# Moving a split store from batch 11 to batch 2 in a batched matmul

## The chip, the core and the metric

The kernel runs on one core of one Trainium2 chip. The metric is device time in microseconds of one execution; lower is better. Sixteen DMA engines serve the core and carry all traffic between its on-chip memory and HBM. Transfers are put on three queues: ACT's (q10 in the profile), SP's (q1) and GpSimd's, called POOL here (q0).

## The reference

```python
batch, m, k, n = 16, 512, 512, 512
a: (batch, m, k) float32, b: (batch, n, k) float32
np.matmul(a, b.transpose(0, 2, 1)).astype(np.float32)
```

Sixteen products of 512 x 512 matrices, each with its second matrix transposed. 33.5 MB are read and 16.8 MB written.

## The kernel before

The batches are worked on in eight pairs. One load brings the two matrices `a` of a pair, the next the two matrices `b`, 2 MB each, into one of `NL = 7` slots of `ld`: 128 partitions, one run of 16 KB in each. Loads 0, 2, 3, ... are put on ACT's queue and load 1 on SP's (`load`, line 86). The first seven go out at the start; ACT issues loads 7 and 8 after its copies `ta` of pair 0, loads 9 and 10 after those of pair 1, and so on.

For each pair DVE casts the halves of `a` and `b` to bf16 (`ha`, `wa`, `hb`, `wb`), PE transposes them in blocks of 128 x 128 into PSUM (`tp`, line 223), ACT copies the transposed `a` to `ta` (line 181) and DVE the transposed `b` to `tb` (line 168). PE multiplies (line 242), and ACT copies the product from PSUM to one of `NO = 7` slots of `ob` (line 201). DVE doesn't wait for a load itself: POOL waits for each load in turn and counts up `s_go` (line 108), and DVE takes one from this count for each load. So whatever stands between two of POOL's waits stands between DVE and the next load.

SP stores the batches in order. It first waits until load 7 has landed (line 120, the second use of slot 0), then for each batch until ACT has copied it (`s_out`), and puts one transfer of 1 MB on its queue: 128 partitions, a run of 8 KB in each (`store`, line 96). ACT waits for the store of batch n - 7 before it writes batch n into the same slot of `ob` (`landed`, line 93, and line 198). The last 256 KB of batch 15 are a transfer of their own at the very end.

One batch is stored in another way, `X = 11`. Of its four rows `j` in each partition, SP stores rows 1 and 2 of all partitions, rows 0 and 3 of partitions 32 to 95, and rows 0 and 3 of partitions 0 to 19 in five transfers of four partitions. POOL, after its last wait for a load, stores rows 0 and 3 of partitions 20 to 31 and 96 to 127 in four rounds of three transfers (lines 112 to 118). Each round begins with a small load of 640 bytes to a scratch tile, `turn`, of five partitions with two runs of 64 bytes, and goes on with a store of three partitions and one of eight. The pieces count on `s_x` (SP's) and `s_y` (POOL's), for which ACT waits at the very end.

Of the kernel before, what the change touches and what calls it, by code (L numbers as in the profile page):

```python
# [10 lines left out]
def kernel(  # L11
# [6 lines left out]
    nc = tc.nc  # L18
    P = 128
    batch, M, K = a.shape  # L20
    _, N, _ = b.shape
    J = M // P
    KO = K // P
    HP = P // 2
    HK = K // 2
    pairs = batch // 2
    f32 = mybir.dt.float32
    bf16 = mybir.dt.bfloat16
    NL = 7
    NO = 7  # L30
    X = 11

    def sbuf(name, shape, dtype):
        return ctx.enter_context(nc.sbuf_tensor(name, shape, dtype))

    def sem(name):
        return tc.alloc_semaphore(name)

    with tc.tile_critical(no_gpsimd_drain=True):  # L41
# [6 lines left out]
        ta = sbuf("ta", [P, KO, 2 * J * P], bf16)  # L48
        tb = sbuf("tb", [P, KO, 2 * J * P], bf16)
        ob = sbuf("ob", [P, NO, J, N], f32)  # L50
        turn = sbuf("turn", [P, 4, 2, 16], f32)
        tp = ctx.enter_context(nc.psum_tensor("tp", [P, 4, 2 * J, P], bf16))
        ps = ctx.enter_context(nc.psum_tensor("ps", [P, 4, N], f32))

# [2 lines left out]
        s_st = [sem(f"s_st{i}") for i in range(NO)]  # L57
# [13 lines left out]
        s_out = sem("s_out")  # L71
        s_x = sem("s_x")
        s_y = sem("s_y")
# [5 lines left out]
            out=ident[:], in_=ident[:], compare_op=mybir.AluOpType.not_equal, fill=1.0,  # L79
# [6 lines left out]
        def load(n, engine):  # L86
            u, slot = n // 2, n % NL
            src = (a if n % 2 == 0 else b)[2 * u:2 * u + 2].rearrange(
                "e (p j) k -> (e p) j k", j=2 * J
            )  # L90
            engine.dma_start(ld[:, slot], src).then_inc(s_ld[slot], 16)

        def landed(n):
            return s_st[n % NO], 16 * (n // NO + 1)

        def store(n, lo=0, hi=J, step=1, part=slice(0, P), engine=nc.sync):
            rows = slice(lo, hi, step)
            return engine.dma_start(  # L98
                out[n].rearrange("(p j) n -> p j n", j=J)[part, rows], ob[part, n % NO, rows]
            )  # L100

        load(0, nc.scalar)
# [3 lines left out]

        for n in range(2 * pairs):
            nc.gpsimd.wait_ge(s_ld[n % NL], 16 * (n // NL + 1)).then_inc(s_go, 1)

        nc.gpsimd.wait_ge(s_out, X + 1)
        for i in range(4):
            nc.gpsimd.dma_start(  # L114
                turn[:5, i], a[0, :5, :64].rearrange("p (x k) -> p x k", x=2)[:, :, :16]
            ).then_inc(s_y, 16)
            for part in (slice(20 + i, 32, 4), slice(96 + i, P, 4)):
                store(X, step=J - 1, part=part, engine=nc.gpsimd).then_inc(s_y, 16)

        nc.sync.wait_ge(s_ld[0], 32)  # L120
        for n in range(batch):
            nc.sync.wait_ge(s_out, n + 1)
            if n != X:
                store(n, hi=J if n < batch - 1 else J - 1).then_inc(landed(n)[0], 16)
                continue


            store(n, lo=1, hi=J - 1).then_inc(landed(n)[0], 16)
            store(n, step=J - 1, part=slice(32, 96)).then_inc(s_x, 16)
            for i in range(4):  # L130
                store(n, step=J - 1, part=slice(i, 16, 4)).then_inc(s_x, 16)
            store(n, step=J - 1, part=slice(16, 20)).then_inc(s_x, 16)

        def taker(engine):
            return lambda s, n: engine.wait_ge(s, n).then_inc(s, -n)  # L135
# [9 lines left out]
        with nc.Fori(0, pairs, engines=[dve]) as u:  # L145
            for x, (h, w, s_c, s_w) in enumerate(
# [4 lines left out]
                if x == 0:  # L151
# [4 lines left out]
                    out=h[:, J:, :], in_=src[:, J:, :HK]  # L156
                ).then_inc(s_c, 1)
                nc.vector.tensor_copy(out=w[:], in_=src[:, :, HK:]).then_inc(s_w, 1)  # L158
            for ko in range(KO):
# [5 lines left out]
                if ko == 1:  # L165
# [3 lines left out]
                    out=tb[:, ko, :],  # L169
# [7 lines left out]
        for u in range(pairs):  # L177
            for ko in range(KO):
                nc.scalar.wait_ge(s_ta, KO * u + ko + 1)
                for e in range(2):  # L180
                    c = nc.scalar.copy(  # L181
                        out=ta[:, ko, e * J * P:(e + 1) * J * P].rearrange(
                            "k (j p h) -> k j p h", j=J, h=2
                        ),
                        in_=tp[:, ko % 2, :, e * HP:(e + 1) * HP].rearrange(
                            "k (h j) p -> k j p h", h=2
                        ),
                    )
                c.then_inc(s_ea, 1)


            for n in (2 * u + NL, 2 * u + NL + 1):
                if n < 2 * pairs:
                    load(n, nc.scalar)
            for e in range(2):
                n = 2 * u + e
                if n >= NO:
                    nc.scalar.wait_ge(*landed(n - NO))
                for j in range(J):
                    nc.scalar.wait_ge(s_mm, J * n + j + 1)  # L200
                    c = nc.scalar.copy(  # L201
                        out=ob[:, n % NO, j, :].rearrange("m (p j) -> m p j", j=2 * J),
                        in_=ps[:, j, :].rearrange("m (j p) -> m p j", j=2 * J),
                    )
                    if e == 0:
                        c.then_inc(s_pv, 1)
                    elif j in (0, J - 1):
                        c.then_inc(s_out, 1)
# [45 lines left out]


    with tc.tile_critical(sync_engine=act, no_gpsimd_drain=True):
        nc.scalar.wait_ge(s_x, 16 * 6)
        nc.scalar.wait_ge(s_y, 16 * 12)
        for n in range(batch - NO, batch):
            nc.scalar.wait_ge(*landed(n))  # L260
    waits = nc.cur_bb.bb.instructions[-1]
# [38 lines left out]
```

## Time and profile before

| | |
|---|---|
| median of 9 runs | 125.01 us (124.77 to 125.44) |
| the profiled execution | 125.01 us |
| its span | 123.2 us |
| PE, DVE, ACT, POOL busy | 91.4, 68.0, 67.9, 8.5 us |
| packets of DMA | 50.35 MB, mean 409 GB/s |
| q10, q1, q0 | 31.46, 18.70, 0.18 MB |
| load 15 counted by POOL | 100.19 us |
| SP issues store 15 | 115.04 us |
| last packet of DMA ends | 121.61 us |

Times within an execution are counted from the start of the span. The page cuts the span in 40 slices of 3.08 us; a digit is the busy share of a slice in tenths. A row of a timeline gives its start, its length, engine, line, operation, what it writes and reads, how many were merged, and in brackets the idle time before it and what ended that. "ACTq" and "SPq" are issues of transfers, which take the issuing engine's time and not that of the transfer.

### The profile page before, as it was taken

The numbers are of one execution on the slowest core, as the hardware profiler recorded it, in microseconds if no ns is written. First come the engines' busy times: TensorE is split into PE (matmuls) and PEld (weight loads), VectorE is DVE, ScalarE is ACT, GpSimd is POOL, SyncE is SP. The second block draws the span as 40 slices with busy tenths as digits, with TensorE's granted clock in tenths as the row PEclk, the third lists the DMA queues.
The fourth block names the chain that finished last, engine by engine and source line by source line (L and its number), as shares of the span: only waits on it lengthen the run. The fifth ranks groups of instructions, "written<-read, shape, count | busy, mean of one in ns | idle before, by whom it ended". The sixth has DMA issues, their size and how long they took to land. (4 is left out here: it accounts for less than half of the span.)

```text
span 123.2 us, 2255 instructions
## 1 busy us (share of the span) xinstructions
PE 91.4 (74%) x768; PEld 56.1 (46%) x768; DVE 68.0 (55%) x96; ACT 67.9 (55%) x130; POOL 8.5 (7%) x18
## 2 busy tenths in 40 slices
PE   0000089999999899989998999999699926999100
PEld 0000078347744764674476447645564425844000
DVE  0000598983895689289918974871987039600000
ACT  0400065468855966796589469765765184645300
POOL 2000000000000000000000000000000029930000
PEclk9999999999999999999999999999999999599965
DMA  4999999999999999999999999999999999999992
GB/s 149 415 426 426 442 426 426 431 426 426 426 426 426 436 340 388 428 439 420 434 431 420 444 423 426 447 420 412 444 428 436 412 426 426 419 405 425 426 420 104
DMA packets 5341, 50.35 MB, mean 409 GB/s; under 512 B 904, under 2 KB 904, under 8 KB 1500
## 3 DMA queue, kind: packets, MB, share of 16 engines
q10 hardware_dynamic: 2160, 31.46, 60.7%
q1 hardware_dynamic: 2796, 18.70, 36.2%
q0 software_dynamic: 384, 0.18, 0.5%
q14 instruction: 1, 0.01, 0.0%
HBM read 33.56 MB, written 16.78 MB: 409 GB/s over the span
## 5 line engine op out<-in xcount | busy, mean ns | idle before, releaser
L242 PE MATMUL ps<-tb,ta 128*128 128x512 bf16 x256 | 58.1, 381 | 0.4
L201 ACT COPY ob<-ps 128x512 f32<-128x512 f32 x64 | 34.3, 590 | 27.4 <-PE ps L242 23.5
L181 ACT COPY ta<-tp 128x512 bf16<-128x512 bf16 x64 | 33.0, 613 | 15.5 <-PE tp L223 15.1
L242 PEld LDWEIGHTS ps<-tb,ta 128*128 128x128 bf16 x256 | 24.4, 98 | 30.6 <-issue 4.1
L223 PE MATMUL tp<-ident,ha 128*128 128x128 bf16 x256 | 18.9, 228 | 18.6 <-PEq L135 18.1
L223 PEld LDWEIGHTS tp<-ident,ha 128*128 128x128 bf16 x256 | 16.2, 102 | 22.1 <-issue 20.5
L168 DVE COPY tb<-tp 128x1024 bf16<-128x1024 bf16 x32 | 21.4, 686 | 4.3 <-DVEq L135 4.3
L223 PE MATMUL tp<-ident,hb 128*128 128x128 bf16 x256 | 18.4, 229 | 3.9 <-PEq L135 3.6
L223 PEld LDWEIGHTS tp<-ident,hb 128*128 128x128 bf16 x256 | 16.2, 103 | 5.0 <-issue 4.7
L154 DVE CAST ha<-ld 128x1024 bf16 x8 | 5.5, 691 | 14.5 <-DVEq L135 14.5
L163 DVE COPY ha<-wa 128x2048 bf16<-128x2048 bf16 x8 | 5.5, 692 | 12.2 <-DVEq L135 12.2
L154 DVE CAST hb<-ld 128x1024 bf16 x8 | 5.5, 690 | 8.8 <-DVEq L135 8.8
L158 DVE CAST wa<-ld 128x2048 bf16 x8 | 9.8, 1221 | 0.0
L158 DVE CAST wb<-ld 128x2048 bf16 x8 | 9.8, 1220 | 0.0
L114 POOL DMA_DIRECT2D turn<-in_a_dram x4 | 2.6, 662 | 99.3 <-DMA ld<-in_b_dram 99.3
L155 DVE CAST hb<-ld 128x1024 bf16 x8 | 5.5, 686 | 0.0
L155 DVE CAST ha<-ld 128x1024 bf16 x8 | 5.5, 686 | 0.0
L167 DVE COPY hb<-wb 128x2048 bf16<-128x2048 bf16 x8 | 5.5, 684 | 0.0
L98 POOL DMA_DIRECT2D out_dram<-ob x8 | 5.2, 650 | 0.0
L176 ACT ACT_TABLE_LOAD x1 | 1.3, 1283 | 4.1 <-issue 4.1
L78 POOL TENSOR_SCALAR_AFFINE_SELECT ident<-ident 128x128 bf16<-128x128 bf16 x1 | 0.3, 288 | 0.2 <-POOL ident L76 0.2
L76 POOL MEMSET ident<- 128x128 bf16 x1 | 0.2, 204 | 0.5 <-SPq L41 0.5
(5 smaller groups left out, 0.6 us busy)
## 6 DMA issues: line engine op xcount, KB each, us to landing
ld<-in_a_dram ACTq DMA_DIRECT2D x8, 2048.0 KB, 29.6
ld<-in_b_dram ACTq DMA_DIRECT2D x7, 2048.0 KB, 27.3
out_dram<-ob SPq DMA_DIRECT2D x14, 1024.0 KB, 28.8
ld<-in_b_dram SPq DMA_DIRECT2D x1, 2048.0 KB, 12.4
out_dram<-ob SPq DMA_DIRECT2D x1, 768.0 KB, 6.4
out_dram<-ob SPq DMA_DIRECT2D x1, 512.0 KB, 24.6
out_dram<-ob SPq DMA_DIRECT2D x2, 256.0 KB, 6.3
out_dram<-ob POOLq DMA_DIRECT2D x4, 32.0 KB, 5.8
```

The source lines that it names most:

```text
L98: return engine.dma_start(out[n].rearrange("(p j) n -> p j n", j=J)[part, rows], ob[part, n % NO, rows])
L114: nc.gpsimd.dma_start(turn[:5, i], a[0, :5, :64].rearrange("p (x k) -> p x k", x=2)[:, :, :16]).then_inc(s_y, 16)
L154: nc.vector.tensor_copy(out=h[:, :J, :], in_=src[:, :J, :HK])
L155: nc.vector.tensor_copy(out=h[:, J:, :], in_=src[:, J:, :HK]).then_inc(s_c, 1)
L158: nc.vector.tensor_copy(out=w[:], in_=src[:, :, HK:]).then_inc(s_w, 1)
L163: nc.vector.tensor_copy(out=ha[:], in_=wa[:]).then_inc(s_ca, 1)
L167: nc.vector.tensor_copy(out=hb[:], in_=wb[:]).then_inc(s_cb, 1)
L168: nc.vector.tensor_copy(out=tb[:, ko, :], in_=tp[:, 2 + ko % 2].rearrange("k j p -> k (j p)"),).then_inc(s_eb, 1)
L181: c = nc.scalar.copy(out=ta[:, ko, e * J * P:(e + 1) * J * P].rearrange("k (j p h) -> k j p h", j=J, h=2), in_=tp[:, ko % 2, :, e * HP:(e ...
L201: c = nc.scalar.copy(out=ob[:, n % NO, j, :].rearrange("m (p j) -> m p j", j=2 * J), in_=ps[:, j, :].rearrange("m (j p) -> m p j", j=2 * J),)
L223: t = nc.tensor.transpose(tp[:, 2 * x + g, j, :], h[:, j, g * P:(g + 1) * P], ident[:])
L242: t = nc.tensor.matmul(ps[:, j, :], ta[:, ko, (e * J + j) * P:(e * J + j + 1) * P], tb[:, ko, :].rearrange("k (j p) -> k j p", j=2 * J)[:, ...
```

## The change

`X` becomes 2, and the batch that is stored in another way is cut by partitions alone: SP stores partitions 0 to 31 and 96 to 127 with all rows, in two transfers of 256 KB; POOL stores partitions 32 to 91 in one transfer of 480 KB and partitions 92 to 95 in another of 32 KB. Ahead of these two POOL does the small load to `turn` once. POOL's three transfers stand in its loop over the loads, after the count for load 7 and before the wait for load 8, and behind a wait for `s_out` of batch 2. Batch 11 is stored by SP in one transfer of 1 MB like the others. ACT waits for the five pieces of batch 2 (`s_x`, `s_y`) before it writes batch 9 to the same slot of `ob`, and not at the end.

```diff
-    X = 11
+    X = 2
...
-        turn = sbuf("turn", [P, 4, 2, 16], f32)
+        turn = sbuf("turn", [5, 2, 16], f32)
...
         def landed(n):
-            return s_st[n % NO], 16 * (n // NO + 1)
+            return s_st[n % NO], 16 * (n // NO + (n % NO != X))
...
         for n in range(2 * pairs):
             nc.gpsimd.wait_ge(s_ld[n % NL], 16 * (n // NL + 1)).then_inc(s_go, 1)
-        nc.gpsimd.wait_ge(s_out, X + 1)
-        for i in range(4):
-            nc.gpsimd.dma_start(
-                turn[:5, i], a[0, :5, :64].rearrange("p (x k) -> p x k", x=2)[:, :, :16]
-            ).then_inc(s_y, 16)
-            for part in (slice(20 + i, 32, 4), slice(96 + i, P, 4)):
-                store(X, step=J - 1, part=part, engine=nc.gpsimd).then_inc(s_y, 16)
+            if n == NL:
+                nc.gpsimd.wait_ge(s_out, X + 1)
+                nc.gpsimd.dma_start(
+                    turn[:], a[0, :5, :64].rearrange("p (x k) -> p x k", x=2)[:, :, :16]
+                ).then_inc(s_y, 16)
+                for part in (slice(HP // 2, HP // 2 + 60), slice(HP // 2 + 60, P - HP // 2)):
+                    store(X, part=part, engine=nc.gpsimd).then_inc(s_y, 16)
...
-            if n != X:
-                store(n, hi=J if n < batch - 1 else J - 1).then_inc(landed(n)[0], 16)
+            if n == X:
+                for part in (slice(0, HP // 2), slice(P - HP // 2, P)):
+                    store(n, part=part).then_inc(s_x, 16)
                 continue
-            store(n, lo=1, hi=J - 1).then_inc(landed(n)[0], 16)
-            store(n, step=J - 1, part=slice(32, 96)).then_inc(s_x, 16)
-            for i in range(4):
-                store(n, step=J - 1, part=slice(i, 16, 4)).then_inc(s_x, 16)
-            store(n, step=J - 1, part=slice(16, 20)).then_inc(s_x, 16)
+            store(n, hi=J if n < batch - 1 else J - 1).then_inc(landed(n)[0], 16)
...
                 n = 2 * u + e
-                if n >= NO:
+                if n == X + NO:
+                    nc.scalar.wait_ge(s_x, 16 * 2)
+                    nc.scalar.wait_ge(s_y, 16 * 3)
+                elif n >= NO:
                     nc.scalar.wait_ge(*landed(n - NO))
...
-        nc.scalar.wait_ge(s_x, 16 * 6)
-        nc.scalar.wait_ge(s_y, 16 * 12)
```

More of the change, by code (lines that the diff above doesn't have):

```diff
@@ L93, in landed, with store @@
         def landed(n):
-            return s_st[n % NO], 16 * (n // NO + 1)
-        def store(n, lo=0, hi=J, step=1, part=slice(0, P), engine=nc.sync):
-            rows = slice(lo, hi, step)
+            return s_st[n % NO], 16 * (n // NO + (n % NO != X))
+        def store(n, lo=0, hi=J, part=slice(0, P), engine=nc.sync):
             return engine.dma_start(
-                out[n].rearrange("(p j) n -> p j n", j=J)[part, rows], ob[part, n % NO, rows]
+                out[n].rearrange("(p j) n -> p j n", j=J)[part, lo:hi], ob[part, n % NO, lo:hi]
             )
```

## The prediction

> **What bounds the kernel now.** I read the 40 slices of the page first, then its queues, then the busy times by stretch, and the timelines of POOL, DVE, ACT and SP around the places the change touches.
>
> ```profile
> DMA  4999999999999999999999999999999999999992
> GB/s 149 415 426 426 442 426 426 431 426 426 426 426 426 436 340 388 428 439 420 434 431 420 444 423 426 447 420 412 444 428 436 412 426 426 419 405 425 426 420 104
> ...
> q10 hardware_dynamic: 2160, 31.46, 60.7%
> q1 hardware_dynamic: 2796, 18.70, 36.2%
> q0 software_dynamic: 384, 0.18, 0.5%
> ```
>
> All sixteen DMA engines are busy from slice 2 to slice 39; no compute engine is above 74%. q10 is ACT's queue (15 loads), q1 is SP's (one load, the stores), q0 is POOL's. So the span is a start of 2.0 us, the work of the DMA engine that ends last, and a tail. A DMA engine is worth a microsecond to the span only if it is that last one.
>
> The busy times by stretch (the last two columns are the DMA share and GB/s):
>
> ```profile
> 42.60:47.20 4.60, 4.46 (x42) 2.62 (x40) 4.15 (x7) 3.33 (x7) 0.00 (x0) 1.00 0.98 335
> 47.20:62.00 14.80, 14.36 (x113) 8.21 (x112) 11.45 (x16) 10.34 (x20) 0.00 (x0) 1.00 1.01 428
> 62.00:99.50 37.50, 35.16 (x310) 21.32 (x307) 23.24 (x33) 24.55 (x49) 0.00 (x0) 1.00 1.01 429
> 99.50:115.00 15.50, 11.55 (x80) 7.09 (x80) 6.21 (x9) 9.77 (x20) 7.82 (x12) 0.89 1.02 420
> ```
>
> There is one hole: from 42.6 to 47.2 us, when SP starts four stores at once beside the running loads, the engines count as busy but move 335 GB/s: 4.60 x (1 - 335/429) = 1.0 us lost by each. From 99.5 to 115, when POOL's queue starts beside stores alone, there is next to none.
>
> To see which DMA engine ends last I took the trace's packet records and strung together, from the end backwards, packets that start 4 ns before the one before ends. Five chains carry the 128-byte packets of `turn`; four of these also carry SP's pieces of four partitions. I call these four engines 0 to 3 and the fifth engine 4. Their last packets end (us) at: engines 0-3 120.86, 120.91, 121.14, 121.49; engine 4 **121.61**; the three with POOL's pieces of 3 partitions (5-7) 120.66, 120.74, 120.92; the other eight (8-15) 120.75 to 121.35. Engine 4 is last although batch 11 gives it least: its 8 KB packets between 101 and 117 us take up to 43 ns more than the 309 of the others, 0.85 us in all; no other engine loses over 0.11 us there. A packet delays its engine by 0.607 us (16 KB), 0.305 (8 KB), 0.155 (4 KB), 0.080 (2 KB) or 0.005 (a semaphore).
>
> **The change part by part.** The profiled execution took 125.01 us (span 123.2 and 1.8 around it), the median of the nine runs; the sum needs no correction.
>
> *Bytes by engine.* Before, batch 11 gives an engine: rows 1-2 8 x 0.155, rows 0 and 3 of 64 partitions 8 x 0.080, then on engines 0-3 ten 2 KB packets, on 5-15 four of 4 KB, on engine 4 none; with the small packets of twelve POOL transfers (0.16) that is 2.87 us on 0-3, 2.05 on 4, 2.63 on 5-15. After, with the 60 partitions dealt onward from the engine after `turn`'s five (5 to 15, then 0 to 3) and the last four on 4 to 7, each engine gets four 8 KB packets from SP; all but engine 4 get four from POOL, 4-7 one more: 2.49 us on 0-3, 1.57 on 4, 2.79 on 5-7, 2.48 on 8-15. Differences -0.38, -0.47, +0.16, -0.15. Added to the ends above, the last ones are 121.11, 121.14, 121.08 and 121.20: by this alone the end moves from 121.61 to 121.20, **-0.41 us**.
>
> *A third queue beside loads.* No row shows POOL's queue starting while loads run. Lower end 0: from 99.5 to 115 its 4 KB packets left no longer packets on fifteen engines. Between: the one 8 KB instruction fetch, at 49.3 us, made the next packet on its engine 0.11 us longer, four times that is 0.44. Upper end: all four packets, 1.22. The nearest row is the hole at 42.6: same place, same packet size, a store queue joining loads; the packet records give 0.93 us an engine there, three 8 KB packets. I take **+0.93 us** on the fifteen engines with four POOL packets, 0.3 on engine 4 with one. No packet later is shorter than its 611 or 309 ns, so such a loss is not won back. Fifteen engines then end at up to 122.13, and they, not engine 4 (121.4), are last.
>
> *POOL.* Twelve transfers go from its end, three (0.95 + 1.74/2 x 2 = 2.7 us, by the rows below) come behind the wait for load 7 at 42.6. Queued behind them is the count for load 8, due at 48.96, which DVE first needs at 56.89. Load 9's count (56.28) is needed at 59.23.
>
> ```profile
> 100.95 0.95 POOL L114 DMA_DIRECT2D turn<-in_a_dram  x1 [99.27 <-DMA ld<-in_b_dram]
> 101.90 1.74 POOL L98 DMA_DIRECT2D out_dram<-ob  x2
> ...
> 56.89 0.69 DVE L154 CAST ha<-ld 128x1024 bf16 x1
> 57.49 0.69 DVE L155 CAST ha<-ld 128x1024 bf16 x1
> 58.09 1.22 DVE L158 CAST wa<-ld 128x2048 bf16 x1
> 59.23 0.69 DVE L154 CAST hb<-ld 128x1024 bf16 x1
> ```
>
> So 2.7 us costs nothing; without the 11 us of cover it would delay pair 4. DVE is busy 4.15 of the 4.60 us in which POOL must now write descriptors, 6.21 of 15.50 before. The Trainium skill (SBUF — State Buffer, "SBUF: two separate sides") says a DVE operation in a two-port mode keeps GpSimd from writing descriptors until it ends, which speaks against this place; by it each transfer might wait one 1.22 us cast more, by the rows none, and either ends before 56.89.
>
> *SP.* Seven issues at 86.7 become one, batch 2 has two for one: store 3 is issued some 0.4 us later behind two megabytes of queued stores, nothing. Stores 3 to 6 land about 2.4 us earlier (half a store less ahead of them, 1.2 us of POOL's packets more), so ACT's two waits on stores (below) go; pair 7 then waits for load 15 as now.
>
> *The new waits.* ACT waits for all five pieces of batch 2 before batch 9 (72.50 us), and behind it are its own copies. SP's half follows stores 0 and 1, which land at 54.4 and 61.7: half a store on and 1.2 us of POOL packets, 67 us, 5 us early. The waits taken from the end were over by 113 us: nothing.
>
> *Loads and the tail.* POOL's packets pass ahead of loads: load 15 lands 1.22 + 0.93 us later. From its landing (100.19) to SP's issue of store 15 (115.04) is 14.85 us; the issue comes at 117.2. DMA work ahead of it lasted to 118.15 on the earliest engine, now 118.9; from an issue to the first packets is 1.05 us (0.92 to 1.97 at the start). Cover left: about 0.7 us on the earliest engine, more on the last.
>
> ```profile
> 98.92 2.05 ACT L201 COPY ob<-ps 128x512 f32<-128x512 f32 x4 [3.13 <-DMA out_dram<-ob]
> ...
> 113.94 1.07 ACT L201 COPY ob<-ps 128x512 f32<-128x512 f32 x2 [0.60 <-PE ps L242]
> ...
> 115.04 1.63 SPq L98 DMA_DIRECT2D out_dram<-ob  x2
> ```
>
> Sum: 121.61 - 0.41 + 0.93 = 122.13, so 125.01 + 0.52 = **125.5 us**.
>
> **The rivals.**
>
> *The third queue joins free* (faster): the cost is 0 as at 101 us, and the end is 121.20: 124.6. It decides below 0.16 us, from which on the change is within 0.25 us of no change, up to 0.66. For it: POOL's packets at 101 to 113 cost nothing. Against: no loads ran then.
>
> *In between* (same): four times the fetch's 0.11 us, 125.0.
>
> *The 60 partitions are not dealt around engine 4* (slower). All of POOL's transfers in this trace have two runs per partition (3, 5 or 8 partitions), and their packets show the dealing going on from one transfer to the next: 5, then 3, then 8 different engines. The new ones have one run of 8 KB, a form that no row shows. If they are dealt from the first engine, engine 4 gets four 8 KB packets: 2.49 for 2.05 us, an end at 122.05, with the queue's cost of 0 to 0.93 125.45 to 126.4. The Trainium skill (DMA: Bandwidth & Descriptors, "Why a DMA increments its semaphore by 16 and not by 1") has both: a round-robin cursor for fewer than 16 engines, and an exception in which GpSimd's direct copies are split into shares of partitions/16 rounded up, 100 partitions on engines 0 to 14; by the cursor the sum is as above, by the exception it is this rival's.
>
> *The compute tail becomes the end* (slower): the half clock of PE (PEclk 5 and 9 in slices 35 and 36) lasts longer as PE waits longer for load 15; from 0.7 us of extra tail on engines run dry, and every us beyond about 1.5 is one us: 126.
>
> **How the numbers follow.** 0.2% (0.25 us) is about what a measurement here can tell from no change. Chances: forecast (the queue's cost near 0.93) 0.37; free join 0.25; in between 0.18; not dealt around engine 4 0.16; tail 0.04. Faster 0.25, same 0.18, slower 0.57. The forecast's own range is 125.3 to 125.9 (costs of 0.7 to 1.22); to hold eight in ten the range takes in the free join and the nearer half of the dealing: 124.6 to 126.1.
>
> **What would show it.** Right: GB/s between 42 and 50 us lower than 335 and 388 for longer; q0 with some 0.5 MB; loads after the eighth landing about 2 us later; the lead of engine 4 as last one gone; ACT's waits on stores gone. Wrong: a stretch from 42.6 to 47.2 at 335 GB/s as now and an end at 121.2 (free join); engine 4 carrying four of POOL's 8 KB packets (dealing); DMA below 9 near 117 us (tail). The base of it all, which engine ended last, is from one execution; engines' ends may lie some 0.3 us otherwise in another.

## The result and the profile after

The changed kernel takes 125.50 us (median of 14 runs, 125.32 to 125.69); the kernel before 125.01 (46 runs). The ratio is 1.0038, 95% interval 1.0028 to 1.0047. The change costs half a microsecond, as forecast, but not for the reasons that the forecast gave.

The busy share of DMA and its rate in 40 slices, and the queues, from the page of the changed kernel:

```profile
DMA  4999999999999999999999999999999999999990
GB/s 143 403 440 430 424 424 430 430 440 435 424 430 424 424 377 398 408 419 435 440 416 435 430 435 419 430 440 424 446 414 430 435 406 424 422 430 427 432 398 27
...
q10 hardware_dynamic: 2160, 31.46, 60.4%
q1 hardware_dynamic: 2544, 18.35, 35.3%
q0 software_dynamic: 144, 0.53, 1.1%
```

POOL's queue now carries 0.53 MB in 144 packets. Slices 15 and 16 (43 to 49 us), in which POOL issues its transfers, are not lower than before (377 and 398 against 340 and 388). POOL's 8 KB packets themselves move from 50.06 to 56.84 us, and there slices 17 and 18 are a little lower than before (408 and 419 against 428 and 439). What differs most is the end: the last slice holds 27 GB/s where it held 104. The busy times by stretch of the changed kernel, the last two columns DMA share and GB/s:

```profile
42.60:47.20 4.60, 4.39 (x43) 2.82 (x44) 4.15 (x8) 3.40 (x8) 1.78 (x3) 1.00 0.98 367
47.20:62.00 14.80, 14.36 (x113) 8.19 (x112) 11.79 (x16) 10.28 (x21) 0.00 (x0) 1.00 1.02 427
62.00:99.50 37.50, 34.99 (x305) 21.10 (x303) 23.30 (x34) 26.15 (x52) 0.00 (x0) 1.00 1.01 428
99.50:115.00 15.50, 12.06 (x91) 7.54 (x88) 6.22 (x9) 8.61 (x17) 0.00 (x0) 0.89 1.01 425
118.00:121.00 3.00, 0.00 (x0) 0.00 (x0) 0.00 (x0) 0.00 (x0) 0.00 (x0) 0.80 0.84 345
121.00:122.00 1.00, 0.00 (x0) 0.00 (x0) 0.00 (x0) 0.00 (x0) 0.00 (x0) 0.50 0.08 31
```

The hole from 42.6 to 47.2 us is smaller than in the first profile of before (367 against 335 GB/s), and 99.5 to 115, now without POOL's transfers, runs at 425 against 420. So fifteen engines gained: stringing the packets together from the end as in the prediction, they end at 119.8 to 121.3 us (before 120.7 to 121.5). From 121.3 on one engine works alone, and it ends at 121.95, where the last one of before ended at 121.61. SP's 8 KB packets between 99 and 117 us are 0.67 us too long in all, in the chain of this engine, as it was with engine 4 before (0.78, counted in the same way). By this mark engine 4 is still last, and by more.

The packet records say why. Ahead of POOL's 8 KB packets each engine of `turn`'s five gets a 128-byte packet, each other engine an 8-byte one; an engine that a transfer passes by gets 4-byte packets in their place. Just one engine shows a run of such 4-byte packets (50.10, 51.02, 51.94, 52.86 us) where the other fifteen have four 8 KB packets each, and it is one with an 8-byte packet, so not engine 4. Followed back from the end to 47.5 us, the chain of the engine that ends last, the one with the long packets, carries four or five of POOL's 8 KB packets, in whichever way packets that end together are told apart. **The 60 partitions do go over fifteen engines, but the one that is spared is not engine 4.**

### The profile page after: what moved, and what is told of

Same layout as the page of the kernel before. It is cut to its first block, busy times and chain, and to the rows that moved or that the text cites. A ratio compares the mean times of both kernels' runs of the same rounds, so it can differ in the third digit from the quotient of the medians.

```text
span 123.5 us, 2240 instructions
## 1 busy us (share of the span) xinstructions
PE 91.9 (74%) x768; PEld 56.9 (46%) x768; DVE 68.1 (55%) x96; ACT 68.0 (55%) x130; POOL 2.5 (2%) x9
## 5 line engine op out<-in xcount | busy, mean ns | idle before, releaser
L220 PE MATMUL tp<-ident,ha 128*128 128x128 bf16 x256 | 19.9, 234 | 17.9 <-PEq L129 17.5
L220 PEld LDWEIGHTS tp<-ident,ha 128*128 128x128 bf16 x256 | 17.2, 106 | 21.4 <-issue 19.5
L113 POOL DMA_DIRECT2D turn<-in_a_dram x1 | 0.8, 757 | 41.7 <-DMA ld<-in_b_dram 41.7
L97 POOL DMA_DIRECT2D out_dram<-ob x2 | 1.0, 520 | 0.0
```

The costliest lines, as they stand in the source:

```text
L97: return engine.dma_start(out[n].rearrange("(p j) n -> p j n", j=J)[part, lo:hi], ob[part, n % NO, lo:hi])
L220: t = nc.tensor.transpose(tp[:, 2 * x + g, j, :], h[:, j, g * P:(g + 1) * P], ident[:])
```

## The experiments

In what follows, engine 4's lag is its last packet's end less the median of the fifteen other ends, read from the packet records of a run's profile. It takes out what delays all engines alike. Before: 0.70 us. Changed kernel: 1.43.

### Dealing around engine 4 after all (two_runs)

POOL's half of batch 2 is sent as rows 0 and 2, then rows 1 and 3, so that each partition has two runs, the form of the stores of before. A second small load, `turn2`, goes ahead of the last store:

```diff
...
+        turn2 = sbuf("turn2", [9, 2, 16], f32)
...
+                sixty = slice(HP // 2, HP // 2 + 60)
+                four = slice(HP // 2 + 60, P - HP // 2)
                 nc.gpsimd.dma_start(
                     turn[:], a[0, :5, :64].rearrange("p (x k) -> p x k", x=2)[:, :, :16]
                 ).then_inc(s_y, 16)
-                for part in (slice(HP // 2, HP // 2 + 60), slice(HP // 2 + 60, P - HP // 2)):
-                    store(X, part=part, engine=nc.gpsimd).then_inc(s_y, 16)
+                store(X, 0, 3, 2, sixty, nc.gpsimd).then_inc(s_y, 16)
+                store(X, 0, 3, 2, four, nc.gpsimd).then_inc(s_y, 16)
+                store(X, 1, 4, 2, four, nc.gpsimd).then_inc(s_y, 16)
+                nc.gpsimd.dma_start(
+                    turn2[:],
+                    a[0, :9, :64].rearrange("p (x k) -> p x k", x=2)[:, :, :16],
+                ).then_inc(s_y, 16)
+                store(X, 1, 4, 2, sixty, nc.gpsimd).then_inc(s_y, 16)
...
```

> The changed kernel, but POOL's half of batch 2 goes in pieces with two runs per partition (rows 0 and 2, then rows 1 and 3), the form that was dealt onward in the trace of before; two small loads set the dealing so that neither piece of 60 partitions touches engine 4. Dealing theory (in the changed kernel the 60 partitions were dealt from the first engine, and engine 4 had its full share): engine 4 has 4 packets of 8 KB and one of 4 KB, 1.47 us against 2.05 before, and ends near 121.1; the last of the others near 121.2 to 121.4; 124.6 to 124.8 us, ratio to before 0.997 to 0.9985. Queue theory (POOL's queue beside loads costs the engines time, whatever they get from it): 125.5 us or more, ratio 1.004, and longer packets between 43 and 57 us than before.

Measured: 124.50 us, ratio 0.9947 (0.9931 to 0.9964); once more, as two_runs_b, 124.53, ratio 0.9964 (0.9950 to 0.9977). Faster than both kernels, and by more than the expectation (0.997 to 0.9985). One of the engines with `turn`'s 128-byte packets, the one with the long packets late in the run, has just one of POOL's 4 KB packets, the others about eight each; the last two engines end together at 121.11, 0.47 after the median. The stretches of two_runs:

```profile
42.60:47.20 4.60, 4.15 (x43) 2.66 (x42) 4.15 (x8) 3.40 (x7) 3.47 (x6) 1.00 0.97 381
47.20:62.00 14.80, 14.35 (x113) 8.22 (x112) 11.86 (x17) 10.28 (x21) 0.38 (x1) 1.00 1.01 424
...
118.00:121.00 3.00, 0.00 (x0) 0.00 (x0) 0.00 (x0) 0.00 (x0) 0.00 (x0) 0.50 0.85 345
121.00:122.00 1.00, 0.00 (x0) 0.00 (x0) 0.00 (x0) 0.00 (x0) 0.00 (x0) 0.50 0.01 4
```

The kernel before at the end:

```profile
118.00:121.00 3.00, 0.00 (x0) 0.00 (x0) 0.00 (x0) 0.00 (x0) 0.00 (x0) 0.50 0.94 388
121.00:122.00 1.00, 0.00 (x0) 0.00 (x0) 0.00 (x0) 0.00 (x0) 0.00 (x0) 0.50 0.10 39
```

After 121 us next to nothing is left (4 GB/s, against 31 in the changed kernel and 39 before): no engine works alone. POOL has six transfers here where loads run; its data packets begin at 50.06 us, and 47.2 to 62 us is at 424 GB/s, against 428 before. The queue theory, which was the forecast's, called for 125.5 us or more and falls.

### Is it the engine, or the form (two_runs_15)?

Only the first small load is taken out of two_runs:

```diff
...
-                nc.gpsimd.dma_start(
-                    turn[:], a[0, :5, :64].rearrange("p (x k) -> p x k", x=2)[:, :, :16]
-                ).then_inc(s_y, 16)
...
-                    nc.scalar.wait_ge(s_y, 16 * 6)
+                    nc.scalar.wait_ge(s_y, 16 * 5)
```

> The run two_runs without its first small load, all else the same: every later transfer is then dealt five engines earlier, so that the two pieces of 60 partitions pass by engine 15 and not by engine 4, which gets 32 KB of them and 4 KB of the small pieces. Theory that sparing engine 4 is what makes two_runs faster: engine 4's end moves back by up to 1.3 us and it is last again, 125.3 to 125.7 us, ratio to before 1.002 to 1.005. Rival, that the gain comes from the form with two runs or from the early place and not from the engine: 124.5 us, ratio 0.995.

> The run two_runs once more, beside two_runs_15 on the same chip. The same kernel: 124.4 to 124.6 us, ratio to before 0.993 to 0.997, and 42.6 to 47.2 us at anything from 365 to 390 GB/s.

> The changed kernel once more on the same chip as two_runs_15: if the form plays no part and only engine 4's share does (64 KB of batch 2 here, 68 KB in two_runs_15), the two have the same time within 0.2 us, 125.4 to 125.6, ratio to before 1.003 to 1.005.

Measured on one chip: two_runs_15 125.61 us (ratio 1.0051, 1.0033 to 1.0070), two_runs_b 124.53, the changed kernel again 125.51 (1.0041, 1.0026 to 1.0056). In two_runs_15 something is left after 121 us again:

```profile
121.00:122.00 1.00, 0.00 (x0) 0.00 (x0) 0.00 (x0) 0.00 (x0) 0.00 (x0) 0.50 0.06 23
```

The same form at the same place is as slow as the changed kernel once it no longer passes by engine 4; the lag is 1.48 us again. 1.1 us hang on a load of 640 bytes whose only use is to set where the next transfer begins. One expectation was missed narrowly: two_runs_b has 363 GB/s from 42.6 to 47.2 us, not 365 to 390. With form and place kept, the share of engine 4 decides; form and place do not gain without it.

### Which engine is the slow one (spare15)?

In the kernel before, the first small load covers four partitions, not five:

```diff
-                turn[:5, i], a[0, :5, :64].rearrange("p (x k) -> p x k", x=2)[:, :, :16]
+                turn[:5 - (i == 0), i], a[0, :5 - (i == 0), :64].rearrange("p (x k) -> p x k", x=2)[:, :, :16]
```

> The kernel before, with its first small load over four partitions and not five, so that POOL's stores of batch 11 are dealt to engines 4 to 14 and engine 15 is spared in place of engine 4. The bytes and the transfers are the same. Theory that engine 4 is slower than the others: it gets its four 4 KB packets back, 0.62 us, and ends near 122.2; 125.6 us, ratio 1.004 to 1.005. Rival (engine 4 was last in one execution by chance, which engine is spared makes no difference): 125.0 us, ratio 1.000.

Measured: 125.74 us, ratio 1.0043 (1.0026 to 1.0060). Sparing another engine by the same bytes helps nothing and costs 0.66 us by the medians, 0.54 by the ratio; the last engine's lag is 1.62. That engine 4 is last is no chance of one execution.

### No part for POOL (plain)

The changed kernel with batch 2 as one transfer of SP:

```diff
-            return s_st[n % NO], 16 * (n // NO + (n % NO != X))
+            return s_st[n % NO], 16 * (n // NO + 1)
...
-            if n == NL:
...
-                nc.gpsimd.wait_ge(s_out, X + 1)
...
-            if n == X:
-                for part in (slice(0, HP // 2), slice(P - HP // 2, P)):
-                    store(n, part=part).then_inc(s_x, 16)
-                continue
...
```

> The changed kernel without POOL's three transfers: batch 2 is one transfer by SP like every other batch, so that all sixteen engines get the same bytes. Dealing theory: engine 4 has 8 packets of 8 KB of it, 2.45 us, the same as in the changed kernel (2.49) and 0.40 more than before; it ends near 121.95; 125.4 to 125.5 us, ratio to before 1.003 to 1.004. Queue theory: without the third queue the cost is gone, and the time falls back to that of before or 0.2 us above, ratio 1.000 to 1.002.

Measured: 125.24 us, ratio 1.0012 (0.9999 to 1.0024), lag of engine 4 1.17 us. Between the two expectations. So of the 0.5 us of the change, by the ratios, about 0.15 comes with batch 11, which no longer relieves engine 4 (worked out at 0.40; why it is less was not tried), and about 0.3 with POOL's transfers of batch 2. These give engine 4 nearly what it has in plain (2.49 us of batch 2 against 2.45, by the prediction's prices), so its share explains only 0.05 of the 0.3. Part of the rest may be the loads' packets that POOL's packets lengthen (see before_again); it is not shown.

### Where the last four partitions go (no_four, no_turn)

no_four leaves the last four partitions of POOL's half unwritten:

```diff
...
-                for part in (slice(HP // 2, HP // 2 + 60), slice(HP // 2 + 60, P - HP // 2)):
+                for part in (slice(HP // 2, HP // 2 + 60),):
...
```

> The changed kernel without POOL's last transfer: partitions 92 to 95 of batch 2 are not stored at all (32 KB of the output are left out). It asks which engines got these four packets. If they went to the four first engines (dealt from the first engine too), engine 4 is still last and the time stays at the changed kernel's, 125.5 us, ratio to before 1.004. If one of them went to engine 4 (dealt from where the transfer before it ended), its end is 0.31 us earlier: 125.2 us, ratio 1.001 to 1.002. Queue theory: 0.3 us less on four engines, the last of fifteen others unchanged, 125.5.

Measured: 125.36 us, ratio 1.0021 (1.0009 to 1.0032), lag 1.34. Between the two cases; the intervals of this ratio and of the changed kernel's overlap.

no_turn drops the small load ahead of POOL's two stores and counts `s_y` to 32.

> The changed kernel without the small load to the scratch tile ahead of POOL's two stores. Dealing theory: the store of 60 partitions with one run each starts at the first engine whatever came before, engine 4 has its four packets and the small load did nothing: 125.4 to 125.5 us, ratio to before 1.002 to 1.004, and the engine that ends last gets four of POOL's 8 KB packets. If instead the small load sets the dealing, other engines get the last four packets and another one is left out; the time changes only if that is engine 4: 125.0.

Measured: 125.62 us, ratio 1.0048 (1.0031 to 1.0065), lag 1.41. That is a little above the range that was given for no effect (125.4 to 125.5), with runs from 125.16 to 126.14. The small load of the changed kernel does nothing for the time, with one run of 8 KB per partition: the slow engine has its four 8 KB packets with and without it, here clearly without a fifth. Whether in the changed kernel a fifth packet lies on engine 4 stays open; the packets of 56 us can't be put to engines without doubt.

### The pieces of two_runs at the old place (late_two_runs)

Batch 11 is stored as two_runs stores batch 2, POOL's six transfers standing after its last wait for a load:

```diff
...
-            store(n, lo=1, hi=J - 1).then_inc(landed(n)[0], 16)
-            store(n, step=J - 1, part=slice(32, 96)).then_inc(s_x, 16)
...
+            store(n, part=slice(0, HP // 2)).then_inc(landed(n)[0], 16)
+            store(n, part=slice(P - HP // 2, P)).then_inc(s_x, 16)
...
```

> The pieces of the run two_runs (32 partitions twice by SP, POOL's half in two runs per partition, dealt around engine 4) at the place of the kernel before: batch 11, POOL's transfers behind its last wait for a load, beside stores alone. Theory that only the bytes of engine 4 count and a third queue costs nothing at either place: 124.5 us as in two_runs, ratio to before 0.994 to 0.997. Theory that the place counts, in that the third queue beside loads costs the fifteen engines up to 0.9 us: here it is saved, 123.8 us, ratio 0.988 to 0.992. Theory that the early place is what gains, since ACT then doesn't wait for stores and the small packets stay away from the tail: back at 125.0, ratio 0.999 or more.

Measured: 126.40 us, ratio 1.0111 (1.0095 to 1.0127). None of the three: it is slower by far more than a gain that is given up. The stretches of late_two_runs around POOL's data (106.9 to 113.3 us):

```profile
99.50:106.00 6.50, 3.90 (x41) 3.78 (x42) 4.93 (x7) 4.58 (x11) 4.69 (x6) 0.74 1.01 424
106.00:113.20 7.20, 7.14 (x42) 3.37 (x40) 1.29 (x2) 4.17 (x8) 0.00 (x0) 1.00 1.02 399
113.20:118.00 4.80, 0.53 (x3) 0.04 (x1) 0.00 (x0) 1.07 (x2) 0.00 (x0) 0.77 1.01 425
```

The middle one in two_runs, and then in the kernel before:

```profile
106.00:113.20 7.20, 7.14 (x47) 3.80 (x46) 1.36 (x3) 4.56 (x10) 0.00 (x0) 0.97 1.01 427
...
106.00:113.20 7.20, 7.20 (x38) 3.70 (x37) 1.38 (x2) 3.65 (x8) 2.77 (x5) 0.88 1.02 414
```

While POOL's packets move beside stores alone, 399 GB/s; two_runs has 427 in the same 7.2 us. SP's 8 KB packets, 309 ns elsewhere, take up to 1,192 there, 7 us over all engines, about 2.5 of it on the engine that ends last. That is engine 4, although it has just one of POOL's 4 KB packets here too: what it is spared in bytes it more than loses in longer packets. So a third queue can have a high price, but here beside stores, and not beside loads as the forecast had it. The pieces of before (3 and 8 partitions, one 4 KB packet per engine at a time) ran at the same place with 414. Why pieces of 60 partitions lengthen the packets of others there was not tried.

### A second look at the kernel before (before_again)

> The kernel before, unchanged, for a second profile: how much of the hole from 42.6 to 47.2 us (335 GB/s in the first profile, 372 in that of spare15, which is the same up to batch 11) belongs to the kernel and how much to one execution. If it belongs to the kernel, 335 again; if to the execution, anything from 335 to 390, and the term that the prediction took from it was no property of a queue's start.

The stretch of the hole in before_again, then in spare15 and late_two_runs, which are the same program up to batch 11:

```profile
42.60:47.20 4.60, 4.46 (x44) 2.74 (x43) 4.15 (x8) 3.40 (x7) 0.00 (x0) 1.00 0.99 365
...
42.60:47.20 4.60, 4.46 (x44) 2.74 (x43) 4.14 (x8) 3.40 (x7) 0.00 (x0) 1.00 0.96 372
...
42.60:47.20 4.60, 4.46 (x44) 2.73 (x43) 4.15 (x8) 3.40 (x7) 0.00 (x0) 1.00 0.97 374
```

So four executions of the same instructions show 335, 365, 372 and 374 GB/s: the hole is there each time, but 335 is the deepest of all twelve profiles and belongs to its execution. plain, without POOL's transfers, has 388, and the seven profiles in which POOL issues its transfers there 363 to 386. But POOL's data packets begin only at 47.5 to 50.6 us, so this stretch can't show what they cost. Counted in packet records from 42 to 60 us, the time by which packets are too long is 0.45 to 0.94 us per engine in the five profiles without POOL there (mean 0.61) and 0.44 to 0.74 in the seven with it (mean 0.61). Counted from 47.2 to 64 us, where POOL's packets move, it is 0.02 to 0.12 us per engine without them, 0.17 to 0.30 in the four profiles with one run per partition, mostly in the loads' 16 KB packets, and 0.08 to 0.15 in the three with two runs. So of the 0.93 us some 0.1 to 0.2 is left in the changed kernel, and with two runs nothing that stands clear. The lag of engine 4 is steadier, 0.78 us in before_again and 0.70 in the first profile.

## Why the prediction was right, and where it was not

The time, the sign and the range were right: 125.5 for 125.50. The sum was not. Two terms were wrong by about 0.8 us each, in opposite directions, and cancelled; that the time came out so close is luck.

*The term -0.41 ("the 60 partitions dealt onward from the engine after `turn`'s five") failed.* The store of 60 partitions with one run each didn't pass by engine 4. By the prediction's own prices engine 4 then has 2.49 us of batch 2 for 2.05 of batch 11, +0.44; its end moved by 0.34 in the profiles, and its lag by 0.73. This is the rival "not dealt around engine 4", at its lower end: 125.45. It had got 0.16; a form of transfer that no row shows deserved more. The Trainium skill (DMA: Bandwidth & Descriptors, "Why a DMA increments its semaphore by 16 and not by 1") has the exception that some of GpSimd's direct copies are cut into shares of partitions/16 rounded up. The traces agree with both of its rules: with the exception for the one-run store, which has shares of four on fifteen engines, with `turn` and without, and with a dealing that goes on from engine to engine for the two-run stores of two_runs. Fifteen engines alone would fit the forecast's dealing too; that the spared one lies outside `turn`'s five does not. Which of the engines outside `turn`'s five is spared, the traces don't show.

*The term +0.93 ("a third queue beside loads") failed.* No profile with POOL's queue there shows it; some 0.1 to 0.2 us may be left of it. The row that it was taken from was the deepest of four executions, and the row that was passed over, POOL's packets costing nothing, came nearer. That row held at its own place for small pieces only: with pieces of 60 partitions late_two_runs takes 1.9 us more than two_runs.

*Engine 4 as the one that ends last* held: spare15 and two_runs_15 show it by their times.

*POOL's step* held: three transfers from 43.39 to 45.17 us (1.8 us, forecast 2.7), the count for load 8 at 48.65, DVE's first use of it at 57.30. POOL's and DVE's timelines of the changed kernel:

```profile
43.39 0.76 POOL L113 DMA_DIRECT2D turn<-in_a_dram  x1 [41.72 <-DMA ld<-in_b_dram]
44.14 1.03 POOL L97 DMA_DIRECT2D out_dram<-ob  x2
...
57.30 0.69 DVE L148 CAST ha<-ld 128x1024 bf16 x1
```

In this profile DVE's casts next to it did not hold POOL up; each store took some 0.5 us to issue. In two_runs_b the four stores took 1.05 us each in the mean; what held them was not looked into.

*The waits of ACT* held in part. Its timeline in the changed kernel:

```profile
97.54 1.07 ACT L198 COPY ob<-ps 128x512 f32<-128x512 f32 x2 [1.13 <-DMA out_dram<-ob]
...
105.64 2.05 ACT L175 COPY ta<-tp 128x512 bf16<-128x512 bf16 x4 [3.81 <-PE tp L220]
...
114.00 1.07 ACT L198 COPY ob<-ps 128x512 f32<-128x512 f32 x2 [0.60 <-PE ps L239]
```

Of 4.0 us of waits on stores 1.1 are left, and what was won became a longer wait for load 15 (3.81 us against 1.58 before), as forecast. No wait for batch 2's pieces shows up before batch 9.

*Loads and tail.* Load 15 is counted at 100.95, 0.76 us later (forecast 2.15, of which 0.93 was the term that failed), and SP issues store 15 at 115.10 (forecast 117.2). The tail's rival had no occasion.

## What to carry to other kernels

Where all DMA engines are busy to the end, ask which one ends last and count its bytes alone: 32 KB on one of sixteen made 1.1 us here, and the changed kernel's DMA share of 1.01 to 1.02 from 47.2 to 115 us showed none of it. A split that is to spare one engine is checked in the packets, since the form of the access pattern (one run per partition or two) decided which engines it went to. A stall seen in one execution is read again in a second one before its depth goes into a sum.

## What the runs showed of the hardware that was not expected

- A small load that has no other use moved the whole kernel by 1.1 us (two_runs_b 124.53, two_runs_15 125.61), by shifting the dealing of POOL's two-run stores by five engines; with one-run stores it moved nothing (no_turn 125.62, the changed kernel 125.51).
- One engine's packets are a few per cent too long in the stretch with stores alone. SP's 8 KB packets from 99 to 117 us are 0.67 to 0.78 us too long in all, in every profile but that of late_two_runs, and most of it lies in one engine's chain (all of it in the changed kernel and in two_runs). What makes it slow was not tried.
- POOL's pieces of 60 partitions with two runs each cost next to nothing beside loads (0.08 to 0.15 us per engine of longer packets, 0.02 to 0.12 without them) and lengthened SP's store packets from 309 to up to 1,192 ns beside stores alone.
- two_runs, 124.5 us, is 0.4 to 0.5% faster than the kernel before.
